# A fourth pair of heads turned through DRAM, other pairs in the output projection's parts, other weight forms: a two-layer decoder trunk on one core

## The chip, the core and the metric

The kernel runs on one core of one Trainium2 chip. The metric is device time in microseconds, the median over several executions. Engines are named as in the profile: PE is TensorE (matrix multiplication), PEld its loading of weights, DVE is VectorE, ACT is ScalarE, POOL is GpSimd, SP is SyncE, which here only issues DMAs.

## What is computed

Two decoder layers on 256 tokens of width 1024 (16 heads of 64), then one RMSNorm. Cut to what matters here:

```python
def reference(x, p, ...):
    h = x
    for i in range(DEPTH):                       # DEPTH = 2
        u = _rmsnorm(h, attn_norm_g[i])
        if i % 2 == 0:                           # layer 0: forgetting attention
            proj = u @ fox_w_in[0]               # q, k, v and the forget gates
            log_f = jax.nn.log_sigmoid(f_logit)
            o = _fox_attention(q, k, v, log_f)   # causal softmax(q.k/8 + c[t] - c[s]) v, c = cumsum(log_f)
            h = h + _merge_heads(o) @ fox_w_o[0]
        else:                                    # layer 1: MoBA; 256 tokens are one block, so it is causal
            proj = u @ moba_w_in[0]              # softmax(q.k/8 + T5 bias) v
            o = _moba_attention(q, k, v, rel_bias_table)
            h = h + _merge_heads(o) @ moba_w_o[0]
        u = _rmsnorm(h, ffn_norm_g[i])
        gu = u @ ffn_w_in[i]                     # 1024 -> 2 x 2816
        h = h + (jax.nn.silu(gu[..., :D_FF]) * gu[..., D_FF:]) @ ffn_w_out[i]
        gate = jax.nn.sigmoid(_rmsnorm(h, ple_norm_g[i]) @ ple_w_gate[i])
        h = h + gate * (p[i] @ ple_w_up[i])
    return _rmsnorm(h, final_norm_g)
```

All is in float32.

## The kernel before

**Products.** Activations lie with features on partitions: `[128, feature block, 256 tokens]`. A float32 product is made of three matmuls of a faster float32 type (`mm3`, L92 to L94): each operand is split into a rounded part `hi` and a remainder `lo`, and hi·hi, hi·lo and lo·hi are added up in a PSUM bank. A chunk of weights (512 KB) is 8 blocks of 128x128, and makes 24 matmuls.

**Weights** stream from DRAM in the order in which the host has laid them out, one chunk at a time, by SP's queue. ACT makes `whi` of a chunk (L164 or L182, one instruction), DVE makes the remainder `wlo` (L166 or L183). There are six buffers of each. A chunk lies in its buffers in one of three forms. Plain, `blocks()`: eight blocks one after the other, from column 16. Gapped, `gapped()`: the first block shifted by 8 columns and the seven others by 64, with 56 columns of zeros between, which come from DRAM with the chunk; `KICK` names the projection's parts that have it. Entry, `blocks(ENTRY)`: `whi` plain, and in `wlo` the first two blocks shifted by 8 and the others by 64, for which DVE makes two instructions of the remainder.

**Attention** (`attention`, the same code for both layers) goes by pairs of heads, 0 to 7. `project(j, 0)` and `project(j, 1)` make q and k of pair j into the bank `pq` (24 matmuls each). DVE scales them by the norm (`qkt`, L514); ACT and DVE split them (`qkh` L523, `qkl` L525). `scores` makes the logits `sp` of one or two pairs: in layer 0 a matmul with `sel` adds the decay (L372), then come q·k in three steps (L540, L543); DVE adds mask or bias and finds the minimum (L554), ACT takes the exponential (L558) into `e`. The probabilities must then be divided by their sum and transposed. There are two roads. For the pairs in `TURNED` = 0, 1, 3, ACT divides (`scaled`, L588, four instructions), DVE transposes 32x32 squares (`turn`, L595, two), POOL's queue writes the tile to DRAM (`dt`, L598) and reads it back in another order by four gathers (`pt`, L601). For the other pairs DVE divides (`normal`, L579, two), PE makes six transposes (`transposes`, L616), and ACT copies them out of PSUM (L623). Tiles `pt` of the DRAM road have two buffers, which a transposed pair without the tag "fp" uses too; the pairs with "fp" use four others. `values(...)` multiplies by v into a bank `po` per pair (L633, L635); ACT and DVE split the result into `o` (L285, L286).

**Order.** Pairs are projected two at a time, scores follow one pair behind, and the transposes and values of earlier pairs stand between a projection and the scores. Then comes the output projection `wo(hf, c)` in eight parts: half `hf` of the outputs, part `c` of the pairs of heads, part c taking the pairs 2c and 2c+1. Between parts stand what remains of the attention:

```
(0,0) | scores 7 | (1,0) | values 3, transposes 5 | (0,1) | transposes 6, 7 | (1,1) |
values 4 5, values 6 7 | (0,2) (1,2) (0,3) (1,3)
```

The program gives a priority by order of writing; `issue_after` and `held` put an instruction behind a named other one. Each engine runs its instructions in order. PSUM has eight banks, which all tiles of `bank(...)` take in turn, so a matmul into a new bank waits for whatever read that bank eight tiles earlier.

Of the kernel before, what the change touches and what calls it, by code (L numbers as in the profile page):

```python
# [32 lines left out]
P = 128  # L33
S = 256
D = 1024
KT = D // P
H = 16
DH = 64
NP = H // 2
DFF = 2816  # L40
FT = DFF // P
# [5 lines left out]
HW = 1024  # L47
HC = 512
# [1 line left out]
WARM = 8  # L50
RAW = 6
RVW = 384
TURNED = (0, 1, 3)


LINE = 64
# [2 lines left out]

FURTHER = 8  # L60
ENTRY = (0, 1)
KICK = ((0, 0), (0, 1), (1, 1), (0, 2))

GAP = LINE - FURTHER
WW = HW + GAP
# [8 lines left out]
def trunk(ctx: ExitStack, tc: tile.TileContext, xg, wx, xr, pt, w, cst, gf, rel, hot, rvm, out):  # L74
# [94 lines left out]
    def blocks(entry=()):  # L169

        hi, lo = half(APART, len(entry) * P)
        return [[t[k] if isinstance(t, list) else t[:, k * P:(k + 1) * P] for k in range(KT)] for t in (hi, lo)]
# [150 lines left out]
    moba = []  # L323
# [103 lines left out]
    def attention(layer, nm, mid, early, nf):  # L427
        vb = [bank(f"v{layer}_{b}") for b in range(4)]
        rest, ahead = None, []
        for c in range(4):  # L430
            wt = [early.pop(0) if early else half() for _ in range(2)]
# [59 lines left out]
        def project(j, a):  # L491
            with held(j - 2):
                if ahead:
                    hi, lo = ahead.pop(0)
                elif j > 2 and (j % 2 == 0 or layer and j == 5) and a == 0 or layer and j == 4:
                    hi, lo = gapped()
                else:
                    hi, lo = blocks(ENTRY if layer and j in (0, 2) and a == 0 else ())
            if a == 0:
                pq[j] = bank(f"pq{layer}_{j}")  # L500
            bk = pq[j]
            for k in range(KT):
                mm3(bk[:, a * S:(a + 1) * S], (hi[k], lo[k]), nm.k(k),
                    start=(k == 0), stop=(k == KT - 1))
            if a == 0:
                return
            del pq[j]
            far = [x for x in fresh if x[0] in TURNED]
            near = [x for x in fresh if x[0] not in TURNED]
            fresh.clear()  # L510
            for x in far:
                scaled(*x)
            t = work.tile([P, 2, S], F32, tag="qkt", bufs=3, name=f"qkt{layer}_{j}")
            got = nc.vector.tensor_tensor(t.rearrange("p a s -> p (a s)"), bk,  # L514
                                          nm.row.rearrange("p a s -> p (a s)"), op=ALU.mult)
            for x in near:
                with tc.issue_after(got.ins):
                    got = normal(*x)

            th = work.tile([P, 3 * P], F32R, tag="qkh", bufs=3, name=f"qkh{layer}_{j}")  # L520
            tl = work.tile([P, 3 * P], F32R, tag="qkl", bufs=3, name=f"qkl{layer}_{j}")
            src = t.rearrange("p a s -> p (a s)")[:, P:]
            first = nc.scalar.activation(th, src, AF.Copy)  # L523
            with tc.issue_after(got.ins):
                got = nc.vector.tensor_tensor(tl, src, f32(th), op=ALU.subtract)  # L525
            marks[j] = first, got
            qk[j] = t, th, tl
            for x in far:
                with tc.issue_after(got.ins):
                    turn(*x[:2])  # L530

        def scores(*js):

            rows = [slice(s * DH, (s + 1) * DH) for s in range(2)]
            heads = [(2 * j + s, d, qk[j], bank(f"sp{layer}_{2 * j + s}")) for j in js for s, d in enumerate(rows)]
            if add:
                for i, _, _, sp in heads:
                    add(i, sp)
            for _, d, (t, _, _), sp in heads:
                mm(sp[:, 0:P], t[d, 0, 0:P], t[d, 1, 0:P], start=add is None, stop=True, skip_group_check=True)  # L540
            for n, (q, k) in enumerate(((1, 1), (1, 2), (2, 1))):
                for _, d, t, sp in heads:
                    got = mm(sp[:, P:3 * P], t[q][d, 0:P], t[k][d, P:], start=False, stop=n == 2,  # L543
                             skip_group_check=True)
            sl = (slice(0, P), slice(P, 3 * P))
            for n, j in enumerate(js):
                del qk[j]
                e = work.tile([P, 2, 3 * P], F32, tag="e", bufs=4, name=f"e{layer}_{j}")

                mn = tiny.tile([P, 2, 2, 2], F32, tag="mn", bufs=4, name=f"mn{layer}_{j}")  # L550
                for s in range(2):
                    i, _, _, sp = heads[2 * n + s]
                    for q, b in enumerate(bias(i)):
                        nc.vector.tensor_tensor_reduce(e[:, s, sl[q]], sp[:, sl[q]], b, 1.0, 3.0e38,  # L554
                                                       ALU.add, ALU.min, mn[:, 0, s, q:q + 1])
                for s in range(2):
                    for q in range(2):
                        last = nc.scalar.activation(e[:, s, sl[q]], e[:, s, sl[q]], AF.Exp, scale=-1.0,  # L558
                                                    bias=mn[:, 0, s, q:q + 1], accum_out=mn[:, 1, s, q:q + 1])
                if j < NP - 3:  # L560
                    fresh.append((j, e, mn))
                else:
                    marks[-j] = last, normal(j, e, mn)
            return got
# [44 lines left out]
        def transposes(j, tag="pt"):  # L609

            e = sm.pop(j)
            for s in range(2):
                i = 2 * j + s
                pp = bank(f"pp{layer}_{i}")
                for q in range(3):
                    got = nc.tensor.transpose(pp[:, q * P:(q + 1) * P], e[:, s, q * P:(q + 1) * P], ident)  # L616
                if tag == "pt":
                    if s == 0:
                        both = work.tile([P, 2, 3 * P], F32, tag="pt", bufs=2, name=f"pt{layer}_{j}")
                    t = both[:, s]  # L620
                else:
                    t = work.tile([P, 2 * S], F32, tag="fp", bufs=4, name=f"pt{layer}_{i}")[:, 0:3 * P]
                nc.scalar.activation(t, pp[:, 0:3 * P], AF.Copy)  # L623
                pts[i] = t.rearrange("p (b c x) -> p b c x", b=3, x=32)
            return got

        def values(*js):

            pos = [bank(f"po{layer}_{j}") for j in js]
            heads = [(slice(s * DH, (s + 1) * DH), slice((2 * j + s) * DH, (2 * j + s + 1) * DH), pts.pop(2 * j + s), po)  # L630
                     for j, po in zip(js, pos) for s in range(2)]
            for d, c, t, po in heads:
                mm(po[d, :S], v[:, 0, c], t[:, 0:2], start=True, stop=False, skip_group_check=True)  # L633
            for d, c, t, po in heads:
                got = mm(po[d, P:S], v[:, 1, c], t[:, 2], start=False, stop=True, skip_group_check=True)  # L635
            for j, po in zip(js, pos):
                marks["o"] = split(oh[:, j], ol[:, j], po[:, :S])
            return got


        for j in range(0, NP, 2):
            for i in (j, j + 1):
                project(i, 0)
                project(i, 1)
            if j >= 4:
                transposes(j - 2, "fp")
                values(*range(max(j - 5, 0), j - 3))
            got = scores(*range(max(j - 1, 0), min(j + 1, NP - 1)))
            if layer == 0 and j == 0:
                with tc.issue_after(got.ins):  # L650
                    moba.extend(moba_bias())

        wb = [[bank(f"wo{layer}_{hf}_{b}") for b in range(2)] for hf in range(2)]

        def wo(hf, c, after):
            with held(after):
                wt = gapped() if (hf, c) in KICK else blocks()
            return cross(wb[hf], wt, (2 * c, 2 * c + 1), lambda k: (oh[:, k], ol[:, k]), 0, KT - 1, c == 3)

        def behind(ins, after, *parts):  # L660
            with tc.issue_after(ins.ins):
# [6 lines left out]
            end = scores(NP - 1)  # L668
        got = behind(end, 6, (1, 0))
        with tc.issue_after(got.ins):  # L670
            values(3)
            got = transposes(5, "fp")
        got = behind(got, 7, (0, 1))
        with tc.issue_after(got.ins):
            transposes(NP - 2)
            got = transposes(NP - 1)
        got = behind(got, -6, (1, 1))
        with tc.issue_after(got.ins):
            values(4, 5)
            got = values(6, 7)  # L680
        got = behind(got, -7, (0, 2), (1, 2))
        behind(got, "o", (0, 3))
# [268 lines left out]
def _gapped(a, first=0):  # L951

    t = a.reshape(P, KT, P)[:, _entered(first)].reshape(P, HW)
    return np.concatenate([t[:, :P], np.zeros((P, GAP), t.dtype), t[:, P:]], axis=1)


def _turned(a):

    t = a.reshape(a.shape[:-1] + (2, 4, 4, 32))
    return np.swapaxes(t, -3, -2).reshape(a.shape)  # L960
# [13 lines left out]

def _wide(a, c, hf):

    t = a[c * P:(c + 2) * P, hf * HC:(hf + 1) * HC]
    return t.reshape(2, P, HC).transpose(1, 0, 2).reshape(P, HW)


def _buckets():
# [84 lines left out]
```

## Time and profile before

| what | value |
|---|---|
| median of 3 executions | 647.32 us (647.26 to 648.54) |
| the profiled execution, its time | 647.72 us |
| its span in the trace | 645.9 us |
| its granted TensorE clock, mean | 0.996 |
| layer 0, from the projection of pair 2 to the end of the output projection | 41.9 to 115.1 us in the span |
| the same of layer 1 | 358.2 to 428.9 us |

Times of the trace are counted from the start of the span; the executions' times contain the span and 1.8 us around it. PE's busy time counts a matmul until its modelled end, and the next one starts before that: the durations of 0.28 us overlap, and what a matmul costs is the step from its start to the next start, some 0.12 us for 128x256. Where a row gives an instruction with "xN", its start is the first one's and its duration covers all N. In brackets stands how long the engine was idle before, and what it waited for.

### The profile page before, as it was taken

To read this page: it belongs to the slowest core of one execution; us is meant where nothing else is said; L and a number is where in the kernel's file an instruction comes from. 1 tells how busy PE (TensorE), PEld (TensorE's weight loads), DVE (VectorE), ACT (ScalarE), POOL (GpSimd) and SP (SyncE) were. 2 spreads that over 40 slices of the span, in tenths; PEclk is the share of its full clock that TensorE was granted. 3 is DMA by queue.
4 is the path that set the end of the run, shared out by engine and by line. 5 is a ranking of instruction groups with operands and counts; after the bars stand their busy time and mean duration, and the time that the engine had idled before them with its cause. 6 is when DMAs were issued, how large, how long until landed. Compare 5 with 4: busy or idle time off the path is not lost.

```text
span 645.9 us, 13154 instructions
## 1 busy us (share of the span) xinstructions
PE 636.6 (99%) x5321; PEld 614.3 (95%) x5321; DVE 454.7 (70%) x734; ACT 375.6 (58%) x645; POOL 26.6 (4%) x53
## 2 busy tenths in 40 slices
PE   9999999999999999999999999999999999999995
PEld 7899989999999999999989999999999999999984
DVE  6778885786666666668893798697666666666685
ACT  6677675764444444448664687676444444454653
POOL 0101110000000000000000031000000000000001
PEclk9999999999999999999999999999999999999998
DMA  8847665497765666665574587366766666666523
GB/s 333 315 137 212 201 181 155 166 332 270 247 202 198 197 195 214 196 206 180 189 247 176 176 251 217 106 232 205 222 198 199 198 196 191 195 207 189 189 97 100
DMA packets 39166, 131.06 MB, mean 203 GB/s; under 512 B 4576, under 2 KB 8640, under 8 KB 39104
## 3 DMA queue, kind: packets, MB, share of 16 engines
q1 hardware_dynamic: 37040, 124.87, 59.7%
q0 software_dynamic: 1632, 4.72, 2.5%
q8 instruction: 42, 0.69, 0.4%
q10 hardware_dynamic: 432, 0.62, 0.3%
q14 instruction: 20, 0.16, 0.1%
HBM read 125.71 MB, written 7.63 MB: 206 GB/s over the span
## 4 chain that ended last, share of the span: by engine, by line
PE 94%; issue 3%; DVE 1%; ACT 1%; POOL 0%; POOLq 0%; DVEq 0%; DMA 0%
PE gu L92 12%; PE gu L93 12%; PE gu L94 12%; PE fo L94 6%; PE fo L93 6%; PE fo L92 6%; PE pq L92 5%; PE pq L94 5%; PE pq L93 5%; PE v L423 4%; PE wo L92 2%; PE wo L93 2%; PE wo L94 2%; PE pg L92 2%; PE pg L93 1%
## 5 line engine op out<-in xcount | busy, mean ns | idle before, releaser
L166 DVE TENSOR_TENSOR wlo<-raw,whi 128x1024 fp32r<-128x1024 f32 (+1 forms) x166 | 200.5, 1216 | 71.3 <-ACT whi L164 65.8
L164 ACT ACTIVATE whi<-raw 128x1024 fp32r<-128x1024 f32 x164 | 172.0, 1057 | 103.4 <-issue 49.8
L92 PE MATMUL gu<-g,whi 128*128 128x256 f32 x704 | 195.2, 277 | 0.0
L93 PE MATMUL gu<-g,whi 128*128 128x256 f32 x704 | 194.9, 277 | 0.0
L94 PE MATMUL gu<-g,wlo 128*128 128x256 f32 x704 | 194.8, 277 | 0.0
L94 PEld LDWEIGHTS gu<-g,wlo 128*128 128x128 f32 x704 | 132.3, 188 | 0.0
L92 PEld LDWEIGHTS gu<-g,whi 128*128 128x128 f32 x704 | 132.3, 188 | 0.0
L93 PEld LDWEIGHTS gu<-g,whi 128*128 128x128 f32 x704 | 132.2, 188 | 0.0
L94 PE MATMUL fo<-fp,wlo 128*128 128x256 f32 x352 | 97.5, 277 | 0.0
L92 PE MATMUL fo<-fp,whi 128*128 128x256 f32 x352 | 97.4, 277 | 0.0
L93 PE MATMUL fo<-fp,whi 128*128 128x256 f32 x352 | 97.4, 277 | 0.0
L183 DVE TENSOR_TENSOR wlo<-raw,whi 128x1080 fp32r<-128x1080 f32 x44 | 55.9, 1275 | 29.7 <-ACT whi L182 29.1
L92 PE MATMUL pq<-g,whi 128*128 128x256 f32 x256 | 71.7, 280 | 0.0
L94 PE MATMUL pq<-g,wlo 128*128 128x256 f32 x256 | 71.0, 277 | 0.0
L93 PE MATMUL pq<-g,whi 128*128 128x256 f32 x256 | 71.0, 277 | 0.0
L93 PEld LDWEIGHTS fo<-fp,whi 128*128 128x128 f32 x352 | 66.2, 188 | 0.0
L92 PEld LDWEIGHTS fo<-fp,whi 128*128 128x128 f32 x352 | 66.1, 188 | 0.0
L94 PEld LDWEIGHTS fo<-fp,wlo 128*128 128x128 f32 x352 | 66.1, 188 | 0.0
L182 ACT ACTIVATE whi<-raw 128x1080 fp32r<-128x1080 f32 x44 | 48.1, 1100 | 27.5 <-PE gu L93 25.4
L92 PEld LDWEIGHTS pq<-g,whi 128*128 128x128 f32 x256 | 48.2, 188 | 1.0 <-issue 0.2
L93 PEld LDWEIGHTS pq<-g,whi 128*128 128x128 f32 x256 | 48.1, 188 | 0.1
L94 PEld LDWEIGHTS pq<-g,wlo 128*128 128x128 f32 x256 | 48.1, 188 | 0.0
(188 smaller groups left out, 999.9 us busy)
## 6 DMA issues: line engine op xcount, KB each, us to landing
raw<-w SPq DMA_DIRECT2D x169, 512.0 KB, 4.2
raw<-w SPq DMA_DIRECT2D x44, 540.0 KB, 4.5
d<-d SPq DMA_DIRECT2D x4, 768.0 KB, 7.0
dt<-turn POOLq DMA_DIRECT2D x6, 384.0 KB, 3.1
pt<-dt POOLq DMA_DIRECT2D x24, 96.0 KB, 5.3
bias<-d SPq DMA_DIRECT2D x4, 512.0 KB, 6.6
dh<-end SPq DMA_DIRECT2D x2, 512.0 KB, 2.6
ut<-dh SPq DMA_DIRECT2D x8, 128.0 KB, 3.2
```

Of the source, the lines that this page charges most:

```text
L92: mm(o, ah, bh, start=start, stop=False, skip_group_check=True)
L93: mm(o, ah, bl, start=False, stop=False, skip_group_check=True)
L94: return mm(o, al, bh, start=False, stop=stop, skip_group_check=True)
L164: state["hi"] = state[f"hi{i}"] = nc.scalar.activation(hi[:, c], raw[:, c], AF.Copy)
L166: nc.vector.tensor_tensor(lo[:, c], raw[:, c], f32(hi[:, c]), op=ALU.subtract)
L182: nc.scalar.activation(ht, raw[:, 0:WW], AF.Copy)
L183: nc.vector.tensor_tensor(lt, raw[:, 0:WW], f32(ht), op=ALU.subtract)
L423: got = mm(bks[2 * t + hf], x[a][:, t * P:(t + 1) * P], w[b][:, hf * HC:(hf + 1) * HC], start=k + a + b == 0, stop=k + b == KT, skip_group ...
```

## The change

Pair 2 joins the pairs that go through DRAM, in both layers. The projection's parts take the pairs 0 1, 2 4, 3 5 and 6 7; the host lays the weights out accordingly. The values of pair 4 move ahead of the last scores in the loop, behind those of pairs 1 and 2; the values of pair 3 move from between two parts to the place that pair 4 had, beside pair 5. The bias of layer 1 (one matmul `pb`, one DVE instruction, one DMA) moves from behind the first scores to ahead of them. Five chunks get other forms: `project(2, 0)` of layer 0 plain to entry; part (0,2) of layer 0 gapped to plain; parts (0,0) and (1,1) of layer 1 gapped to plain; part (0,2) of layer 1 gapped to entry. The transposes of pair 7 use the buffers "fp". Lines below L62 move down by one.

```diff
-TURNED = (0, 1, 3)
+TURNED = (0, 1, 2, 3)
...
-KICK = ((0, 0), (0, 1), (1, 1), (0, 2))
+KICK = (((0, 0), (0, 1), (1, 1)), ((0, 1),))
+PARTS = ((0, 1), (2, 4), (3, 5), (6, 7))
...
-                    hi, lo = blocks(ENTRY if layer and j in (0, 2) and a == 0 else ())
+                    hi, lo = blocks(ENTRY if (layer or j) and j in (0, 2) and a == 0 else ())
...
+            if layer + j == 0:
+                moba.extend(moba_bias())
             if j >= 4:
-                transposes(j - 2, "fp")
+                if j - 2 not in TURNED:
+                    transposes(j - 2, "fp")
                 values(*range(max(j - 5, 0), j - 3))
+            if j == NP - 2:
+                values(4)
             got = scores(*range(max(j - 1, 0), min(j + 1, NP - 1)))
-            if layer == 0 and j == 0:
-                with tc.issue_after(got.ins):
-                    moba.extend(moba_bias())
...
-                wt = gapped() if (hf, c) in KICK else blocks()
-            return cross(wb[hf], wt, (2 * c, 2 * c + 1), lambda k: (oh[:, k], ol[:, k]), 0, KT - 1, c == 3)
+                wt = gapped() if (hf, c) in KICK[layer] else blocks(ENTRY if layer and (hf, c) == (0, 2) else ())
+            return cross(wb[hf], wt, PARTS[c], lambda k: (oh[:, k], ol[:, k]), 0, KT - 1, c == 3)
...
         with tc.issue_after(got.ins):
-            values(3)
             got = transposes(5, "fp")
         got = behind(got, 7, (0, 1))
         with tc.issue_after(got.ins):
             transposes(NP - 2)
-            got = transposes(NP - 1)
+            got = transposes(NP - 1, "fp")
         got = behind(got, -6, (1, 1))
         with tc.issue_after(got.ins):
-            values(4, 5)
+            values(3, 5)
             got = values(6, 7)
...
 def _wide(a, c, hf):
 
-    t = a[c * P:(c + 2) * P, hf * HC:(hf + 1) * HC]
-    return t.reshape(2, P, HC).transpose(1, 0, 2).reshape(P, HW)
+    t = a.reshape(-1, P, D)[list(c), :, hf * HC:(hf + 1) * HC]
+    return t.transpose(1, 0, 2).reshape(P, HW)
```

**DVE at pair 4, layer 0.** In the rows, a name's last number only tells one tile from another; the number before it is the pair (`e_2` is pair 2), and for weights there is none. This is DVE before, from pair 4's `qkt` to pair 5's; `rc_2` is the reciprocal that pair 2 is divided by:

```order
L514 TENSOR_TENSOR qkt_4_773<-pq_4_712,row_326 128x512
L571 RECIPROCAL rc_2_775<-mn_2_697 128x4
L579 TENSOR_TENSOR e_2_696<-e_2_696,rc_2_775 128x2x128
L579 TENSOR_TENSOR e_2_696<-e_2_696,rc_2_775 128x2x256
L525 TENSOR_TENSOR qkl_4_780<-qkt_4_773,qkh_4_779 128x384
L595 STREAM_TRANSPOSE turn_1_783<-e_1_686 128x3x4x32 x2
L183 TENSOR_TENSOR wlo_925<-raw_923,whi_924 128x1080
L166 TENSOR_TENSOR wlo_956<-raw_954,whi_955 128x1024
L514 TENSOR_TENSOR qkt_5_854<-pq_5_799,row_326 128x512
L525 TENSOR_TENSOR qkl_5_857<-qkt_5_854,qkh_5_856 128x384
```

And now:

```order
L572 RECIPROCAL rc_2_774<-mn_2_698 128x4
L515 TENSOR_TENSOR qkt_4_780<-pq_4_713,row_326 128x512
L526 TENSOR_TENSOR qkl_4_783<-qkt_4_780,qkh_4_782 128x384
L596 STREAM_TRANSPOSE turn_1_786<-e_1_687 128x3x4x32 x2
L596 STREAM_TRANSPOSE turn_2_796<-e_2_697 128x3x4x32 x2
L184 TENSOR_TENSOR wlo_926<-raw_924,whi_925 128x1080
L167 TENSOR_TENSOR wlo_957<-raw_955,whi_956 128x1024
L515 TENSOR_TENSOR qkt_5_867<-pq_5_812,row_326 128x512
L287 TENSOR_TENSOR o_369<-po_0_873,o_369 128x256
L526 TENSOR_TENSOR qkl_5_870<-qkt_5_867,qkh_5_869 128x384
```

The two dividing instructions of pair 2 are gone from ahead of `qkl_4`, and its two turns stand ahead of the next weights' remainder; on ACT four divisions of pair 2 now stand ahead of `qkh_4`.

**POOL, layer 0.** This is the queue of the DRAM road before, for pairs 1 and 3:

```order
L598 DMA dt_1_786<-turn_1_783 128x768
L601 DMA pt_1_788<-dt_1_786 32x4x192 x4
L598 DMA dt_3_1003<-turn_3_1000 128x768
L601 DMA pt_3_1005<-dt_3_1003 32x4x192 x4
L243 TENSOR_TENSOR col_1632<-ms_1630,nhalf 128x2
```

And now:

```order
L599 DMA dt_1_789<-turn_1_786 128x768
L599 DMA dt_2_799<-turn_2_796 128x768
L602 DMA pt_1_791<-dt_1_789 32x4x192 x4
L602 DMA pt_2_801<-dt_2_799 32x4x192 x4
L599 DMA dt_3_1004<-turn_3_1001 128x768
L602 DMA pt_3_1006<-dt_3_1004 32x4x192 x4
```

Pair 2's copy out stands between pair 1's copy and its gathers, and pair 2's gathers behind those.

**PE at the projection's first part, layer 0.** This is the change of bank within part (0,0) before, with the semaphores that an instruction waits for ("Activation" is ACT; `wo0_0_0` is layer 0, half 0, bank 0):

```order
L94 MATMUL wo0_0_0_1155<-o0_369,wlo24_1161 128x256
L92 MATMUL wo0_0_1_1156<-o0_369,whi24_1160 128x256 [waits Activation_49]
L93 MATMUL wo0_0_1_1156<-o0_369,whi24_1160 128x256
L94 MATMUL wo0_0_1_1156<-o0_369,wlo24_1161 128x256
L92 MATMUL wo0_0_1_1156<-o0_369,whi24_1160 128x256
```

And now:

```order
L95 MATMUL wo0_0_0_1163<-o0_369,wlo24_1169 128x256
L93 MATMUL wo0_0_1_1164<-o0_369,whi24_1168 128x256 [waits DVE_49]
L94 MATMUL wo0_0_1_1164<-o0_369,whi24_1168 128x256
L95 MATMUL wo0_0_1_1164<-o0_369,wlo24_1169 128x256
L93 MATMUL wo0_0_1_1164<-o0_369,whi24_1168 128x256
```

The second bank is six matmuls behind the first, and is now freed by DVE where an ACT eviction freed it.

More of the change, by code (lines that the diff above doesn't have):

```diff
@@ L1012 @@
                 for n, a in enumerate(_cols(wi[:, :D], wi[:, D:2 * D]))]
-        seq += [_gapped(_wide(wo, 2 * c, hf)) if (hf, c) in KICK else _wide(wo, 2 * c, hf)
+        seq += [_gapped(_wide(wo, PARTS[c], hf)) if (hf, c) in KICK[i] else _wide(wo, PARTS[c], hf)
                 for hf, c in ((0, 0), (1, 0), (0, 1), (1, 1), (0, 2), (1, 2), (0, 3), (1, 3))]
@@ L1024 @@
                 seq += o[f - 2:f]
-        seq.append(_wide(fout[i], FT - 4, 0))
+        seq.append(_wide(fout[i], (FT - 4, FT - 3), 0))
         seq += _rows(_turned(ar(ple_w_up)[i]) if i else ar(ple_w_up)[i])
-        seq += [_wide(fout[i], f, hf) for f, hf in ((FT - 2, 0), (FT - 4, 1), (FT - 2, 1))]
-        a = [_wide(_turned(ar(ple_w_gate)[i]) if i else ar(ple_w_gate)[i], 2 * c, hf) for hf in range(2) for c in range(4)]
+        seq += [_wide(fout[i], (f, f + 1), hf) for f, hf in ((FT - 2, 0), (FT - 4, 1), (FT - 2, 1))]
+        a = [_wide(_turned(ar(ple_w_gate)[i]) if i else ar(ple_w_gate)[i], (2 * c, 2 * c + 1), hf) for hf in range(2) for c in range(4)]
         seq += a if i else [_gapped(t) for t in a]
```

## The prediction

> **What bounds the kernel now.** I read the page's busy times and its chain first, then who waited for whom on TensorE, then windows by stage of the attention, and last the timelines of TensorE (PE), VectorE (DVE), ScalarE (ACT) and GpSimd (POOL) around the places that the diff touches.
>
> ```profile
> PE 636.6 (99%) x5321; PEld 614.3 (95%) x5321; DVE 454.7 (70%) x734; ACT 375.6 (58%) x645; POOL 26.6 (4%) x53
> PE 94%; issue 3%; DVE 1%; ACT 1%; POOL 0%; POOLq 0%; DVEq 0%; DMA 0%
> PE wo L92 <- ACT o L285: 0.5, 1, 0.5
> PE wo L93 <- DVE o L286: 0.3, 1, 0.3
> ```
>
> PE is busy for 99% of the span and carries 94% of the chain that ends last, so the time is the sum of PE's rows plus the few places where PE waits. Only one place of any size is listed: the output projection, once for ACT's half and once for DVE's half of an attention output `o`. A change pays here if it takes rows off PE or takes a wait away, and costs if it gives PE a new wait. Whether it can do the latter is told by how full the helpers are where the change adds work:
>
> ```profile
> 69.38:84.31 14.93, 14.93 (x145) 14.16 (x143) 12.33 (x31) 10.93 (x30) 1.34 (x3) 1.00 0.69 200
> 103.72:115.14 11.42, 11.42 (x99) 11.42 (x97) 10.63 (x15) 9.20 (x14) 0.00 (x0) 1.00 0.64 208
> ```
>
> These are layer 0's stage of pairs 6 and 7, and the projection's last four parts (columns: length, PE, weight loads, DVE, ACT, POOL, clock, DMA share, GB/s). DVE has 12.33 of 14.93 us filled in the first and 10.63 of 11.42 in the second: it runs close behind PE, and late work on it is caught up slowly.
>
> **The weight form of pair 2, layer 0.** Layer 1 already has there, behind the same kind of score matmuls, the "entry" form that layer 0 now gets.
>
> ```profile
> 41.91 0.39 PE L92 MATMUL pq<-g,whi 128*128 128x256 f32 x1
> 53.20 0.28 PE L94 MATMUL pq<-g,wlo 128*128 128x256 f32 x1
> 53.41 0.62 PE L372 MATMUL sp<-c,sel 64*128 64x384 f32 x4
> 358.22 0.39 PE L92 MATMUL pq<-g,whi 128*128 128x256 f32 x1
> 369.33 0.72 PE L540 MATMUL sp<-qkt 64*128 64x128 f32 x8
> ```
>
> The 96 matmuls of pairs 2 and 3 take 41.91 to 53.41 = 11.50 us in layer 0, and 358.22 to 369.33 = 11.11 us in layer 1. I take the whole difference, -0.39 (ends 0 and -0.5). The bias matmul `pb`, which now stands ahead of the first scores and no longer between them and pair 2, takes there what it took here and costs nothing anew; its one DVE instruction moves with it, in a stage where DVE is not yet behind. The second DVE instruction that an entry remainder takes falls there too, and in layer 1 into part (0,2), ahead of which DVE has stood idle while PE makes the values.
>
> **Pair 2 leaves TensorE, in both layers.**
>
> ```profile
> 66.01 0.28 PE L94 MATMUL pq<-g,wlo 128*128 128x256 f32 x1
> 66.13 0.82 PE L616 MATMUL pp<-con,e 128*128 128x128 f32 x6
> 66.88 0.65 PE L633 MATMUL po<-pt,v 128*64 128x256 f32 x4
> 67.68 0.62 PE L372 MATMUL sp<-c,sel 64*128 64x384 f32 x4
> ```
>
> Six transposes fill 66.13 to 66.88 = 0.75. A projection that ends before a 64-row matmul needs 0.21 for its last step (53.20 to 53.41) where it needs 0.12 before a transpose (66.01 to 66.13), so 0.09 comes back: -0.66 a layer, -1.32 in all (ends -1.2 and -1.5). The Trainium skill, in "VectorE: DVE Perf Modes", section "The three transpose paths", gives 390 ns for a 128x128 transpose on TensorE and advises TensorE for this size; by that figure twelve of them would be 4.7 us and the sum below nearer -5.9. The trace has 0.125 us each here, and the trace decides.
>
> **Values regrouped.** Pair 3 no longer stands alone between two parts of the projection; pair 4 joins pairs 1 and 2, and pair 3 takes pair 4's old place.
>
> ```profile
> 81.15 1.08 PE L633 MATMUL po<-pt,v 128*64 128x256 f32 x8
> 82.60 0.62 PE L372 MATMUL sp<-c,sel 64*128 64x384 f32 x4
> 91.13 0.65 PE L633 MATMUL po<-pt,v 128*64 128x256 f32 x4
> 91.93 0.88 PE L616 MATMUL pp<-con,e 128*128 128x128 f32 x6
> ```
>
> Alone, a pair takes 0.80 (91.13 to 91.93; 0.80 too at 66.88 to 67.68) and another 0.09 at the edge. Two together take 1.45, so a further one 0.65. Net -0.25 a layer, -0.50 in all (ends -0.3 and -0.7). Pair 4's evictions must be done by then; the six transposes lie 1.45 us of value matmuls ahead, more than ACT's two evictions take.
>
> **The wait in projection part (0,1).** Its second half needs `o` of pair 3, whose value matmuls ran just before.
>
> ```profile
> 93.95 0.28 PE L94 MATMUL wo<-o,wlo 128*128 128x256 f32 x1
> 94.70 0.39 PE L92 MATMUL wo<-o,whi 128*128 128x256 f32 x1 [0.46 <-ACT o L285]
> 95.37 0.39 PE L93 MATMUL wo<-o,whi 128*128 128x256 f32 x1 [0.28 <-DVE o L286]
> 408.91 0.28 PE L92 MATMUL wo<-o,whi 128*128 128x256 f32 x1
> 409.09 0.39 PE L93 MATMUL wo<-o,whi 128*128 128x256 f32 x1
> 409.31 0.28 PE L94 MATMUL wo<-o,wlo 128*128 128x256 f32 x1
> ```
>
> Steps are 0.12 elsewhere in this part; here they are 0.75 and 0.67 in layer 0 (1.18 too long) and 0.18 and 0.22 in layer 1 (0.16 too long). With pairs 2 and 4 the part needs only outputs that are some 7 us old. I take -1.34 (ends -1.1 and -1.5). Next in line are pairs 3 and 5 for part (0,2), behind two value groups as pairs 4 and 5 were, so nothing is late there that was not before.
>
> **What the helpers pay.** Pair 2's scaling goes from DVE to ACT: four more instructions ahead of `qkh` of pair 4, and DVE turns two pairs before it splits the next weights.
>
> ```profile
> 60.75 1.48 ACT L588 ACTIVATE e<-e,rc 128x128 f32<-128x128 f32 x4
> 62.13 0.51 ACT L523 ACTIVATE qkh<-qkt 128x384 fp32r<-128x384 f32 x1
> 63.15 1.03 DVE L595 STREAM_TRANSPOSE turn<-e 128x384 f32<-128x384 f32 x2
> 64.11 1.24 DVE L183 TENSOR_TENSOR wlo<-raw,whi 128x1080 fp32r<-128x1080 f32 x1
> 67.97 0.56 DVE L525 TENSOR_TENSOR qkl<-qkt,qkh 128x384 fp32r<-128x384 f32 x1 [0.89 <-ACT qkh L523]
> 75.16 0.69 DVE L514 TENSOR_TENSOR qkt<-pq,row 128x512 f32<-128x512 f32 x1 [1.28 <-PE pq L94]
> 84.31 0.39 PE L92 MATMUL wo<-o,whi 128*128 128x256 f32 x1
> 84.45 0.75 DVE L286 TENSOR_TENSOR o<-po,o 128x256 fp32r<-128x256 f32 x2
> ```
>
> Four scalings take 62.13 - 60.75 = 1.38, so `qkh`, `qkl` and the first turn come 1.38 later; the second turn adds 64.11 - 63.15 = 0.96. The two normalizing instructions that DVE loses stood ahead of `qkl`, in time that DVE now spends waiting for ACT, so they give nothing back. The weight remainder at 64.11 is thus 2.34 later, 1.95 with the 0.39 that pair 2's form gains. DVE makes up for it out of its idle 0.89 at 67.97 (two evictions of pair 2 no longer stand ahead of that `qkh`) and by one weight remainder that the new order puts behind the score operations, into the 1.28 idle at 75.16; I count some 0.34 left, and from there on DVE has almost no idle time until the projection. What it hits is a PSUM bank. The banks go round by eight, and with three value banks for two, and two transposes' banks gone, the projection's second bank now is the one that DVE's split of pair 1 frees (before, an ACT eviction freed it). That split, the first of the two at 84.45, ended some 0.41 later at 84.86 and now ends at 85.20. PE reaches the first part at 84.31 - 0.39 - 0.66 + 0.65 = 83.91 and the bank six matmuls on, 0.22 and five times 0.12 later, at 84.73: a new wait of 0.47, say 0.5.
>
> ```profile
> 399.25 0.38 PE L92 MATMUL wo<-o,whi 128*128 128x256 f32 x1
> 399.73 0.75 DVE L286 TENSOR_TENSOR o<-po,o 128x256 fp32r<-128x256 f32 x2
> ```
>
> In layer 1 the bank is wanted at 399.25 - 0.66 + 0.65 + 0.82 = 400.06 and was free at 400.14 before. PE has no `sel` matmuls there (the row at 67.68 is one of these groups), so the helpers have less time to catch up: I put the split 0.5 late, which is a wait of 0.6, and 0.1 for pair 7's weights. Together +1.2; the ends are 0 (all caught up) and 2.7 (1.95 late in layer 0 leaves more standing).
>
> **Other weight forms.** Layer 1's parts (0,0) and (1,1) and both tails from (0,2) lose or change the gap. Both tails run at 11.42/96 = 0.119 us a matmul where others have 0.116 or less. Back at that pace a tail would save 0.3 to 0.5, but DVE fills 10.63 of the 11.42, so the feed-forward part would start no more than some 0.1 or 0.2 sooner. I take -0.15 for all four (ends +0.2 and -0.9).
>
> **The road through DRAM.** Per layer five more DMAs on POOL's queue: pair 2's copy out goes between pair 1's copy and its four gathers, and pair 2's gathers stand behind those.
>
> ```profile
> 64.47 0.56 POOL L598 DMA_DIRECT2D dt<-turn  x1 [7.96 <-DVE turn L595]
> 67.64 2.18 POOL L601 DMA_DIRECT2D pt<-dt  x4 [2.60 <-DMA dt<-turn]
> 384.23 2.18 POOL L601 DMA_DIRECT2D pt<-dt  x4 [3.20 <-DMA dt<-turn]
> 396.44 1.08 PE L633 MATMUL po<-pt,v 128*64 128x256 f32 x8
> DMA to landing us min/median/max: 4.0/5.3/6.9
> ```
>
> Layer 0: the copy of pair 1 issues at 64.47 + 1.38 - 0.39 = 65.46, pair 1's gathers at 68.63 to 70.81, pair 2's at 70.81 to 72.99, landed by 79.9 at the slowest; PE wants them at 81.15 - 1.05 = 80.10. Layer 1: issued 384.23 + 1.38 + 2.18 = 387.79 to 389.97, landed at 395.3 in the median and 396.9 at worst, wanted at 396.44 - 0.66 + 0.1 = 395.9. I cost it at nothing; its cover is 0.2 at worst in layer 0 and 0.6 in the median in layer 1, and up to 1.0 if that is gone. Pair 3's gathers now wait for pair 1's buffer too, but are wanted some 10 us later than before.
>
> **Sum.** -0.39 - 1.32 - 0.50 - 1.34 + 1.2 - 0.15 = -2.5 us on the profiled execution of 647.72 (span 645.9 and 1.8 around it). That execution lies 0.40 above the median of 647.32; the change is in the span, so I carry -2.5 to the median: **644.8**.
>
> **Rivals.** (a) The helpers' lateness is not caught up, and the bank waits eat the gain: DVE's fullness speaks for it, its idle 0.89 and 1.28 against. With the upper end of 2.7 for 1.2 the time is 646.3, no measurable change. (b) The paces and the lateness both fall well: helper waits at 0.3 and the tails at full gain give 647.32 - 0.39 - 1.32 - 0.50 - 1.34 + 0.3 - 0.9 = 643.2. (c) The new form at pair 2 does not do in layer 0 what it does in layer 1: without its 0.39 and with nothing from the other forms, 645.3. (d) Slower: pair 2's probabilities come too late for the value matmuls of pairs 1 and 2, and PE stands there in both layers. It costs as much as the landing overshoots 80.1 and 395.9, and decides when the two overshoot by 2.5 together. If each of the eight gathers of pairs 1 and 2 were held up by one DVE instruction of 1.2, pair 2 would be 9.6 later, some 9 us would stand out per layer, and the time were about 662. Against it: the four gathers at 67.64 issued in 2.18, 0.55 each, while DVE worked without a break beside them but for 0.89. The Trainium skill, "SBUF — State Buffer", section "SBUF: two separate sides", warns of exactly this (descriptors of POOL's DMAs blocked by VectorE on a shared port); the 0.55 here shows no such blocking.
>
> **Chances.** Forecast 0.62, (a) 0.11, (b) 0.11, (c) 0.12, (d) 0.04. 0.2% is 1.3 us, about what a measurement of this kernel can tell from no change. Faster by more: forecast, (b), (c) and a little of (a), 0.86; within: the rest of (a), 0.10; slower 0.04. The range leaves out (d), half of (a) and the edge of (b): 643.6 to 646.1.
>
> **What would show it.** Pairs 2 and 3 of layer 0 in 11.1; no transposes behind pair 5; part (0,1) of layer 0 in some 3.0 for 4.19 without a wait on `o`; in the first part of each projection a wait of about half a microsecond, six matmuls in, ended by DVE's `o`. If that wait is over 1 us, or the first value matmul of pair 2 is released by a DMA, or DVE's `qkl` of pair 4 is late by much more than 1.4, the forecast is too low.

## The result

The changed kernel takes 644.25 us (median of 5, 644.07 to 645.16) beside 648.36 of the kernel before in the same group of runs: ratio 0.9947, interval 0.9932 to 0.9961. In a later group it took 644.45 beside 647.53: 0.9951 (0.9937 to 0.9964). Against the 647.32 on which the prediction stood that is -3.1; forecast were -2.5, 644.8, and 643.6 to 646.1. The kernel before took 647.52 to 647.55 in three later groups, so its 648.36 is high, and the gain is some 3.1 to 3.3 us, 0.5%. One execution of the later group took 3646 us and one of share_dve below took 1646; the ratios leave both out.

The profiled execution's span went from 645.9 to 642.5. Of these -3.4, -0.59 lie ahead of pair 2's first matmul in layer 0, which starts at 41.91 before and at 41.32 after. They are there already at the layer's first projection (29.77 and 29.19), ahead of anything that was changed. Over all profiles of this study the start of pair 2 lies between 41.29 and 42.19 and follows no edit; both profiles of the changed kernel have 41.32, and what sets it was not found. So every profile is compared below from that matmul to the end of the span: **603.99 before, 601.18 after, -2.81**. The spans are read to 0.1, so such a difference is good to about 0.1.

### The profile page after: what moved, and what is told of

The parts are those of the page before. It is cut to its first block, busy times and chain, and to the rows that moved or that the text cites. A ratio compares the mean times of both kernels' runs of the same rounds, so it can differ in the third digit from the quotient of the medians.

```text
span 642.5 us, 13152 instructions
## 1 busy us (share of the span) xinstructions
PE 632.9 (99%) x5309; PEld 611.4 (95%) x5309; DVE 454.2 (71%) x736; ACT 376.9 (59%) x649; POOL 32.3 (5%) x63
## 4 chain that ended last, share of the span: by engine, by line
PE 82%; DVE 4%; issue 4%; ACT 4%; DMA 3%; POOL 1%; POOLq 0%; DVEq 0%; ACTq 0%
PE gu L94 13%; PE gu L93 12%; PE gu L95 12%; PE fo L95 6%; PE fo L94 6%; PE fo L93 6%; PE v L424 4%; PE wo L93 2%; PE pq L93 2%; PE wo L94 2%; PE wo L95 2%; PE pq L95 2%; PE pq L94 2%; DMA pt<-dt 2%; PE pg L93 2%
## 5 line engine op out<-in xcount | busy, mean ns | idle before, releaser
L167 DVE TENSOR_TENSOR wlo<-raw,whi 128x1024 fp32r<-128x1024 f32 (+1 forms) x168 | 202.9, 1215 | 71.7 <-ACT whi L165 65.9
L165 ACT ACTIVATE whi<-raw 128x1024 fp32r<-128x1024 f32 x166 | 174.1, 1056 | 103.3 <-issue 49.6
L184 DVE TENSOR_TENSOR wlo<-raw,whi 128x1080 fp32r<-128x1080 f32 x40 | 50.8, 1275 | 28.6 <-ACT whi L183 28.6
L183 ACT ACTIVATE whi<-raw 128x1080 fp32r<-128x1080 f32 x40 | 43.7, 1101 | 26.4 <-PE gu L94 25.4
```

Of the source, the lines that this page charges most:

```text
L165: state["hi"] = state[f"hi{i}"] = nc.scalar.activation(hi[:, c], raw[:, c], AF.Copy)
L167: nc.vector.tensor_tensor(lo[:, c], raw[:, c], f32(hi[:, c]), op=ALU.subtract)
L183: nc.scalar.activation(ht, raw[:, 0:WW], AF.Copy)
L184: nc.vector.tensor_tensor(lt, raw[:, 0:WW], f32(ht), op=ALU.subtract)
```

## The profile after

The page: the span, two of the engines, and the chain that ended last.

```profile
span 642.5 us, 13152 instructions
PE 632.9 (99%) x5309; PEld 611.4 (95%) x5309; DVE 454.2 (71%) x736; ACT 376.9 (59%) x649; POOL 32.3 (5%) x63
PE 82%; DVE 4%; issue 4%; ACT 4%; DMA 3%; POOL 1%; POOLq 0%; DVEq 0%; ACTq 0%
```

PE has lost 3.7 us of busy time and twelve matmuls. The chain, 94% PE before, now leaves PE: where PE waits for a bank, the page follows it back through DVE, ACT and the DMAs (DVE itself shows no wait for a DMA there). PE's waits name the place (us in total, times, longest):

```profile
PE wo L93 <- DVE o L287: 0.7, 2, 0.4
```

That is the wait that was forecast, once in each layer; the waits of 0.5 and 0.3 for `o` in part (0,1) are gone. PE's timeline in layer 0 (start, duration, operation, tiles), the first row of each stage:

```profile
41.32 0.38 PE L93 MATMUL pq<-g,whi 128*128 128x256 f32 x1
52.45 0.44 PE L373 MATMUL sp<-c,sel 64*128 64x384 f32 x2
54.15 0.39 PE L93 MATMUL pq<-g,whi 128*128 128x256 f32 x1
65.25 0.65 PE L634 MATMUL po<-pt,v 128*64 128x256 f32 x4
66.05 0.61 PE L373 MATMUL sp<-c,sel 64*128 64x384 f32 x4
79.52 1.08 PE L634 MATMUL po<-pt,v 128*64 128x256 f32 x8
80.87 0.60 PE L634 MATMUL po<-pt,v 128*64 128x256 f32 x4
81.62 0.61 PE L373 MATMUL sp<-c,sel 64*128 64x384 f32 x4
83.32 0.38 PE L93 MATMUL wo<-o,whi 128*128 128x256 f32 x1
84.03 0.28 PE L95 MATMUL wo<-o,wlo 128*128 128x256 f32 x1
84.62 0.39 PE L93 MATMUL wo<-o,whi 128*128 128x256 f32 x1 [0.32 <-DVE o L287]
91.24 0.36 PE L93 MATMUL wo<-o,whi 128*128 128x256 f32 x1
94.06 0.49 PE L617 MATMUL pp<-con,e 128*128 128x128 f32 x3
```

Pairs 2 and 3 take 52.45 - 41.32 = 11.13 for 11.50 (11.12 by unrounded starts, as in the table below). At 65.25 values follow where six transposes stood. The three value pairs take 81.62 - 79.52 = 2.10. In part (0,0) the seventh matmul starts 0.59 behind the sixth, where 0.12 is the step. Part (0,1) takes 94.06 - 91.24 = 2.82 for 4.19. Layer 1:

```profile
386.89 0.28 PE L94 MATMUL pq<-g,whi 128*128 128x256 f32 x1
387.14 0.38 PE L95 MATMUL pq<-g,wlo 128*128 128x256 f32 x1
397.36 0.28 PE L95 MATMUL wo<-o,wlo 128*128 128x256 f32 x1
397.99 0.38 PE L93 MATMUL wo<-o,whi 128*128 128x256 f32 x1 [0.35 <-DVE o L287]
414.26 0.39 PE L93 MATMUL wo<-o,whi 128*128 128x256 f32 x1
425.27 0.28 PE L93 MATMUL gu<-g,whi 128*128 128x256 f32 x1
425.60 0.39 PE L94 MATMUL gu<-g,whi 128*128 128x256 f32 x1
```

The first two rows are a wait for pair 7's `wlo` (0.25 for a step of 0.11), the next two the bank. The tail takes 425.27 - 414.26 = 11.01 for 11.41, and then the feed-forward part's first step is 0.33, waiting for `g`. What the helpers do behind pair 4 in layer 0:

```profile
59.79 2.87 ACT L589 ACTIVATE e<-e,rc 128x128 f32<-128x128 f32 x8
62.56 0.51 ACT L524 ACTIVATE qkh<-qkt 128x384 fp32r<-128x384 f32 x1
63.10 0.56 DVE L526 TENSOR_TENSOR qkl<-qkt,qkh 128x384 fp32r<-128x384 f32 x1 [2.43 <-ACT qkh L524]
63.58 1.95 DVE L596 STREAM_TRANSPOSE turn<-e 128x384 f32<-128x384 f32 x4
84.16 1.08 DVE L287 TENSOR_TENSOR o<-po,o 128x256 fp32r<-128x256 f32 x3
68.84 4.37 POOL L602 DMA_DIRECT2D pt<-dt  x8 [2.46 <-DMA dt<-turn]
```

ACT makes eight divisions ahead of `qkh`, DVE waits 2.43 for it, and only then turns both pairs. POOL issues the eight gathers in 4.37, 0.55 each, while DVE is busy for 3.79 of the 4.37.

The stages in which before and after differ, from a stage's first matmul to the next one's (us):

| stage | layer 0 before, after | layer 1 before, after |
|---|---|---|
| pairs 2 and 3 | 11.50, 11.12 | 11.11, 11.11 |
| pairs 4 and 5, and the transposes behind them | 11.77, 11.11 | 11.83, 11.17 |
| pairs 6 and 7 | 11.02, 11.02 | 11.02, 11.26 |
| values ahead of the loop's last scores | 1.45, 2.10 | 1.45, 2.10 |
| part (0,0) | 2.95, 3.56 | 3.03, 3.56 |
| part (1,0), then values of 3 and transposes of 5 | 4.35, 3.41 | 4.35, 3.51 |
| part (0,1) | 4.19, 2.82 | 3.06, 2.84 |
| part (1,1) | 2.99, 2.90 | 3.00, 2.91 |
| the last four parts, then the first 72 of the feed-forward | 19.64, 19.63 | 19.62, 19.51 |

The rows add up to -2.7. What follows the 72 matmuls of layer 1, which no edit touches, took 208.7 to 209.1 over all profiles, so differences of less than 0.5 to the end of the span say little by themselves; the stages say more.

## The experiments

Each row's last column is the time from pair 2's first matmul to the end of the span in the profile, 603.99 before and 601.18 after (after_again is the changed kernel once more, in the group of dve_scale, share_dve and double_turn). The ratio is to the kernel before in the same group. The profiled execution of old_parts, 651.23, was the slowest of its six.

| kernel | median | ratio to before | to the end |
|---|---|---|---|
| no_entry | 644.94 | 0.9956 (0.9944 to 0.9969) | 601.14 |
| pb_only | 647.11 | 0.9994 (0.9986 to 1.0003) | 603.83 |
| pb_back | 644.89 | 0.9962 (0.9949 to 0.9974) | 601.51 |
| turned_only | 649.38 | 1.0027 (1.0018 to 1.0036) | 605.41 |
| parts_only | 645.28 | 0.9965 (0.9951 to 0.9978) | 602.11 |
| old_parts | 649.40 | 1.0031 (1.0020 to 1.0043) | 607.96 |
| old_forms | 644.92 | 0.9962 (0.9950 to 0.9975) | 601.73 |
| after_again | 644.45 | 0.9951 (0.9937 to 0.9964) | 601.28 |
| share | 643.77 | 0.9940 (0.9926 to 0.9953) | 600.18 |
| dve_scale | 643.12 | 0.9931 (0.9918 to 0.9943) | 599.95 |
| share_dve | 643.25 | 0.9930 (0.9917 to 0.9944) | 600.02 |
| double_turn | 645.49 | 0.9966 (0.9954 to 0.9978) | 601.98 |

**What made pairs 2 and 3 of layer 0 faster: the form, or the place of `pb`?** Three kernels fill the table of the two edits.

```diff
no_entry, against the changed kernel:
-  blocks(ENTRY if (layer or j) and j in (0, 2) and a == 0 else ())
+  blocks(ENTRY if layer and j in (0, 2) and a == 0 else ())
pb_only, against the kernel before (pb_back is the reverse, against the changed one):
+            if layer + j == 0:
+                moba.extend(moba_bias())
             ...
             got = scores(*range(max(j - 1, 0), min(j + 1, NP - 1)))
-            if layer == 0 and j == 0:
-                with tc.issue_after(got.ins):
-                    moba.extend(moba_bias())
```

> The changed kernel, but project(2, 0) of layer 0 has plain weights again; nothing else differs. Theory A (the form sets PE's pace): the 96 matmuls of pairs 2 and 3 of layer 0 go from 11.12 us back to 11.50, and the span from 642.5 to 642.9. Theory B (the pace came from moving the bias matmul pb from directly ahead of pair 2 to ahead of the scores): they stay at 11.1 and the span at 642.5.

> The kernel before with one edit alone: the bias matmul pb, its DVE instruction and its DMA stand ahead of the first scores of layer 0. Plain weights at pair 2, as before. Theory A (moving pb gave pairs 2 and 3 of layer 0 their faster pace): their 96 matmuls go from 11.50 to 11.1 us, span 645.9 - 0.4 = 645.5. Theory B (the pace there needs the other edits as well, such as another state of PE on entry): 11.5, span 645.9.

> The changed kernel with pb, its DVE instruction and its DMA back behind the first scores, directly ahead of pair 2; the entry form of pair 2 stays. Theory A (the pace comes from where pb stands, and the form does nothing): 11.12 goes to 11.5, span 642.9. Theory B (either of the two edits is enough; with pb ahead of pair 2 the entry form's gap brings the fast pace after eight matmuls, as in layer 1's other entry chunks): 11.1 to 11.15, span 642.5.

Pair 2's first matmul and the first score matmul behind pair 3, PE's timeline. Without the entry form, `pb` moved:

```profile
41.66 0.38 PE L93 MATMUL pq<-g,whi 128*128 128x256 f32 x1
52.76 0.44 PE L373 MATMUL sp<-c,sel 64*128 64x384 f32 x2
```

The kernel before with `pb` moved alone:

```profile
41.77 0.38 PE L92 MATMUL pq<-g,whi 128*128 128x256 f32 x1
52.87 0.44 PE L372 MATMUL sp<-c,sel 64*128 64x384 f32 x2
```

The changed kernel with `pb` back ahead of pair 2, the entry form kept:

```profile
41.92 0.34 PE L393 MATMUL pb<-hot,rr 64*128 64x384 f32 x1
42.19 0.38 PE L93 MATMUL pq<-g,whi 128*128 128x256 f32 x1
53.69 0.44 PE L373 MATMUL sp<-c,sel 64*128 64x384 f32 x2
```

11.10, 11.10 and 11.50. With the changed kernel's 11.12 and the 11.50 of before, the pace follows `pb` in all four cells, and the form does nothing there. In the time, 0.4 us is too little for the intervals; it is the rows that decide.

**What pair 2's road is worth alone, and the new parts alone.** turned_only is the kernel before with `TURNED = (0, 1, 2, 3)` and the transposes of pair 2 left out; parts_only is the kernel before with `PARTS`, `values(4)` and `values(3, 5)` and the buffers of pair 7 as in the change; old_parts is the changed kernel with the parts and values of before.

> The kernel before with one edit alone: pair 2 through DRAM in both layers. Theory A (terms as predicted and seen): twelve transposes with their edges are -1.32; no bank wait arises, since the banks stand as before; helpers run up to 2 us later, which costs about 0.2 at pair 7's weights in layer 1; the wait in part (0,1) stays: span 645.9 - 1.1 = 644.8. Theory B (the helpers' lateness costs more than a bank): the gain is under 0.5, span above 645.4, and PE waits for qkl, weights or o at places where it didn't before.

> The kernel before with the parts and values of the changed one, alone: parts of pairs 0 1, 2 4, 3 5, 6 7, values(4) ahead of the last scores of the loop, values(3, 5) later, pair 7's transposes in the other buffers. Pair 2 stays on TensorE, the weight forms and pb stay. Theory A: values -0.5; the wait for o in part (0,1) goes, -1.3 to -1.5; the new bank wait in part (0,0) comes without any lateness of the helpers from pair 2, so under 0.5 a layer (PE comes 0.65 later, the bank's reader as before): 0.1 to 0.3 each; span 645.9 - 1.5 = 644.4. Theory B (the bank wait is as large as in the changed kernel, because it is the third value pair that makes it): 0.6 and 0.5, span 645.0.

> The changed kernel with the parts and values of before: parts take pairs 0 1, 2 3, 4 5, 6 7; values(3) alone ahead of part (0,1), values(4, 5) later. Pair 2 stays on the DRAM road, the forms stay. Theory A (the new wait in part (0,0) is for the PSUM bank that the third value pair put there): the waits in (0,0) vanish in both layers (3.56 to about 3.0), the wait for o in part (0,1) of layer 0 comes back (2.82 to about 4.2), values cost 0.5 more: span 642.5 + 0.5 + 1.5 - 1.1 = 643.4. Theory B (the wait in (0,0) is the helpers' lateness from pair 2's divisions and turns, whatever the bank): it stays, and the span is about 644.5.

turned_only is slower than before: theory B, and beyond it, since no gain is left at all. The transposes go as forecast (11.11 and 11.17 where 11.77 and 11.83 stood), but part (0,1) grows from 4.19 to 5.03 in layer 0 and from 3.06 to 3.60 in layer 1, (0,0) by 0.23 and 0.42, and some 0.6 more is lost at scores, weights and (1,0). ACT and PE in layer 0 there:

```profile
93.76 0.28 PE L94 MATMUL wo<-o,wlo 128*128 128x256 f32 x1
95.35 0.38 PE L92 MATMUL wo<-o,whi 128*128 128x256 f32 x1 [1.31 <-ACT o L285]
93.99 1.04 ACT L164 ACTIVATE whi<-raw 128x1024 fp32r<-128x1024 f32 x1
94.94 0.36 ACT L285 ACTIVATE o<-po 128x256 fp32r<-128x256 f32 x1
```

PE reaches the need for pair 3's `o` as early as before or earlier, ACT reaches its eviction 0.65 later (94.94 for 94.29); the two weight copies ahead of it stand there before, too, and start 0.64 later themselves (93.99 for 93.35 in the second), so ACT has carried its lateness this far. parts_only makes -1.88 of the -2.81 by itself. Its part (0,0) takes 2.95 and 2.93: no bank wait without pair 2's lateness. So turned_only +1.42, parts_only -1.88 and pb_only's stage -0.40 add up to -0.9; together they make -2.8. Of the missing 1.9, some 1.4 lie in the two attentions and the 72 matmuls behind each. The waits on a fresh `o` in part (0,1), 0.84 and 0.54, which lateness adds in the old parts and cannot add in the new ones, are as much by themselves. The other losses that the changed kernel does not have (0.4 in turned_only at scores and part (1,0), 0.3 in parts_only at layer 0's feed-forward) are for the most part made up by its larger loss in part (0,0), 0.61 and 0.53 where turned_only has 0.23 and 0.42. The last 0.5 lie behind layer 1's attention, within the scatter given above. old_parts was meant as the same test from the other side and is no clean one: it kept pair 7's transposes in the buffers "fp", which pair 4 still holds until its later values, and PE waits 0.8 for ACT's `pt` there; part (0,1) of layer 0 took 5.25.

**Bank or lateness?** share puts the values of pairs 1 and 2 into one bank; dve_scale lets DVE divide pair 2; share_dve does both.

```diff
share:
+            if js == (1, 2):
+                both = bank(f"po{layer}_1")
+                pos = [both[:, n * S:n * S + S] for n in range(2)]
...
-                mm(po[d, :S], v[:, 0, c], t[:, 0:2], start=True, ...)
+                mm(po[d, :S], v[:, 0, c], t[:, 0:2], start=n < 2 or js != (1, 2), ...)
dve_scale:
-            near = [x for x in fresh if x[0] not in TURNED]
+            near = [x for x in fresh if x[0] not in TURNED or x[0] == 2]
...
             for x in far:
-                scaled(*x)
+                if x[0] != 2:
+                    scaled(*x)
```

> The changed kernel, but the values of pairs 1 and 2 share one PSUM bank (256 columns each), so that two banks hold the three pairs and the projection's second bank is one that PE and ACT left long before. Theory A (bank): no wait six matmuls into (0,0); the next need of pair 1's o is six matmuls further on, 0.7 us later, when it is ready; (0,0) takes about 3.0 for 3.56 in both layers, span 642.5 - 1.0 = 641.5, time about 643.2. Theory B (lateness, not the bank): the wait only moves six matmuls on, to the first use of pair 1's o, and the span stays within 0.2 of 642.5.

> The changed kernel, but pair 2 is divided by DVE (reciprocal and two multiplications, as before the change) and not by four ACT instructions, in both layers; it still goes through DRAM. Theory A (the helpers' lateness comes from ACT's four divisions ahead of qkh of pair 4, during which DVE stands idle 2.4 us, so that DVE can divide at no cost): qkl of pair 4, the turns and all gathers come 1.0 to 1.4 earlier, the bank waits in part (0,0) shrink from 0.61 and 0.53 to under 0.2 each, the wait for pair 7's weights in layer 1 goes; from pair 2's first matmul to the end 601.2 - 1.0 = 600.2. Theory B (the lateness is DVE's own, from the two turns): DVE gets 1.0 more work, the waits stay or grow, 601.2 or more.

> The changed kernel with both: pairs 1 and 2 share a value bank, and DVE divides pair 2. Theory A: no wait on banks as in the shared version, pair 7's weights in layer 1 in time (-0.2), the road of pair 2 with about 1 us to spare: from pair 2's first matmul to the end 600.0, some 1.2 less than the changed kernel, time about 643. Theory B (sharing had taken all there was): 600.2, as the shared version.

> The changed kernel once more, as the reference of this group. From pair 2's first matmul to the end 601.2 in the profile; the start before that may differ by up to 0.9, as it did between the runs so far (41.3 to 42.2).

share: part (0,0) takes 2.95 and 2.92 for 3.56, as theory A has it, and PE has no wait left in the projection. 0.2 of the gain is lost elsewhere: layer 1's last four parts ran at 11.41 again and not at 11.01, with the same weight forms. dve_scale has the same 2.95 and 2.92 with the changed kernel's banks, and pair 7's weights in time (11.00 for 11.26). ACT and DVE behind pair 4 of layer 0 in dve_scale:

```profile
60.01 1.48 ACT L590 ACTIVATE e<-e,rc 128x128 f32<-128x128 f32 x4
61.40 0.51 ACT L525 ACTIVATE qkh<-qkt 128x384 fp32r<-128x384 f32 x1
60.96 1.03 DVE L581 TENSOR_TENSOR e<-e,rc 128x256 f32<-128x256 f32 x2
61.94 0.56 DVE L527 TENSOR_TENSOR qkl<-qkt,qkh 128x384 fp32r<-128x384 f32 x1
62.41 1.95 DVE L597 STREAM_TRANSPOSE turn<-e 128x384 f32<-128x384 f32 x4
83.04 1.08 DVE L287 TENSOR_TENSOR o<-po,o 128x256 fp32r<-128x256 f32 x3
```

PE there, the sixth and the seventh matmul of part (0,0), with the step of 0.12 and no wait:

```profile
84.25 0.28 PE L95 MATMUL wo<-o,wlo 128*128 128x256 f32 x1
84.37 0.28 PE L93 MATMUL wo<-o,whi 128*128 128x256 f32 x1
```

DVE's two multiplications lie in time in which it waited for ACT; `qkl` has no wait there, and counted from pair 2's first matmul (41.55 and 41.32) it starts at 20.39 for 21.78. DVE's `o` ahead of part (0,0) is as much earlier, 41.49 for 42.84. So neither the third value bank (parts_only) nor the lateness (share) makes the wait for the bank alone, and it is ACT's four divisions that make the lateness. Lateness alone costs something else: the 0.23 and 0.42 of turned_only in part (0,0) come where pair 1's new `o` is first used, behind the twelfth matmul, in layer 1 as a wait of 0.20 on DVE's `o`, with slower steps after it. dve_scale, 643.12, has the lowest median of all, 1.3 under the changed kernel in the same group (0.9931 and 0.9951, whose intervals just overlap; its slowest execution, 643.63, lies below the changed kernel's fastest, 644.19; 1.3 too from pair 2 to the end); with the shared bank on top (643.25) nothing more is to be had.

**The road through DRAM, and the lateness doubled.** double_turn lets DVE turn pair 1 twice.

```diff
-            for s in range(2):
+            for s in (0, 1, 0, 1) if j == 1 else (0, 1):
                 nc.vector.transpose(...)
```

> The changed kernel, but DVE turns pair 1 twice (two transposes more, same data, in both layers), which puts pair 1's copy out, all eight gathers of pairs 1 and 2 and the DVE work behind it 0.96 us later. Theory A (in layer 0 pair 2's road has no spare time left; in one run of this study PE waited 0.3 for it): the value matmuls of layer 0 wait about 0.9 for pair 2's gathers, and PE then finds the bank of part (0,0) as before; layer 1 has about 1 us to spare on the road and pays at the bank instead, up to 0.9. Together +1.2 to +1.8, span measured from pair 2's first matmul 601.2 to about 602.7. Theory B (the road has spare time and the helpers catch up): under +0.5.

Neither theory holds as written. It costs 0.8 in all, but layer 0 pays 0.1 at the bank and nothing at the gathers. That does not show spare time on the road: counted from pair 2's first matmul the copies went out 0.91 later (24.50 for 23.59), but pair 1's landed sooner, so that the gathers began only 0.13 later (27.65 for 27.52). Nor is DVE's `o` ahead of part (0,0) late by the added 0.96: it starts 0.08 later than in the changed kernel (84.94 - 42.02 for 84.16 - 41.32). So in layer 0 more work of DVE at this place is caught up, and more work of ACT, by dve_scale, is not. Layer 1 pays at pair 7's weights, in PE's timeline:

```profile
388.07 0.28 PE L94 MATMUL pq<-g,whi 128*128 128x256 f32 x1
388.76 0.39 PE L95 MATMUL pq<-g,wlo 128*128 128x256 f32 x1 [0.41 <-DVE wlo L167]
```

The 96 matmuls take 12.26 for 11.26, and with PE that much later the bank is free: (0,0) takes 2.94; the feed-forward part starts 0.3 slower. Here one lateness is paid once, at the first place that is tight. That the road in layer 0 has little to spare was seen elsewhere, in old_forms:

```profile
80.27 0.65 PE L634 MATMUL po<-pt,v 128*64 128x256 f32 x4
81.27 0.65 PE L634 MATMUL po<-pt,v 128*64 128x256 f32 x4 [0.35 <-DMA pt<-dt]
```

Pair 2's values stand 0.5 behind there; its gathers took up to 7.9 us to land, 7.0 in the changed kernel's profile, where PE did not wait. How often that happens was not tried.

**The projection's weight forms.** old_forms is the changed kernel with `KICK` of before in both layers.

> The changed kernel with the projection's weight forms of before in both layers: parts (0,0), (0,1), (1,1) and (0,2) gapped. Theory A (the forms of the projection were worth what the stages show): layer 1's last four parts go from 11.01 back to 11.4, the feed-forward part after it, which waited 0.3 for the norm's g, gets that back; together under 0.3 slower, span 642.5 to 642.8. Theory B (the forms mean nothing here, paces fall as PE happens to enter a stage): no stage changes by more than 0.1 except by chance, and one that was slow may be fast.

Layer 1's tail is slow again (11.41, then 8.21), as theory A has it. But parts_only, with the same forms, has 11.02 and then 8.50 there, the changed kernel's figures with the new forms; and layer 0's tail became fast in both, 11.02 for 11.41, and lost by it. So it is theory B: the pace does not follow the form. The first matmuls of the feed-forward part in parts_only:

```profile
112.37 0.28 PE L93 MATMUL gu<-g,whi 128*128 128x256 f32 x1
112.83 0.38 PE L94 MATMUL gu<-g,whi 128*128 128x256 f32 x1 [0.18 <-DVE g L205]
113.05 0.28 PE L95 MATMUL gu<-g,wlo 128*128 128x256 f32 x1
113.17 0.28 PE L93 MATMUL gu<-g,whi 128*128 128x256 f32 x1
```

PE waits for the norm's `g`, and the 72 matmuls then take 8.92 for 8.22: tail and feed-forward together 19.94, 0.3 more than with the slow tail.

## Why the prediction was right, and where it was not

- **Weight form of pair 2, -0.39: right size by luck, wrong cause.** The stage gave -0.38, because the change moves `pb` as well. The step that failed is the bias matmul that "takes there what it took here and costs nothing anew": moving it is the whole effect, and the form has none. I had compared layer 0 with layer 1 and seen one difference, the form; there was a second, that layer 0 alone had a matmul of another shape directly ahead of the stage. Rival (c) had the form right and the time wrong.
- **Transposes, -1.32: right.** -0.66 in each layer. The Trainium skill's 390 ns a transpose ("VectorE: DVE Perf Modes", "The three transpose paths") would have made -4.7 of it. The page gives it for bf16; the step in this trace's rows of float32 transposes is 0.125, and that is what held.
- **Values regrouped, -0.50: right.** +0.65 at the loop's end and, with the edges at part (1,0), -0.94 and -0.84 behind it: -0.29 and -0.19.
- **Wait in part (0,1), -1.34:** -1.37 and -0.22, in all -1.59; some 0.2 of it is that the part's 24 steps run at 0.113 for 0.118.
- **What the helpers pay, +1.2: right in place and size.** Part (0,0) grew by 0.61 and 0.53, of which the waits six matmuls in, ended by DVE's `o`, are 0.47 and 0.51 over the usual step; with +0.24 at pair 7's weights that is 1.38. But where I had the lateness from ACT's divisions and DVE's turn together, with the divisions taken off ACT nothing is left of the waits, and with DVE's turns doubled layer 0 paid 0.1. The prediction saw that DVE's lost multiplications would give nothing back, since DVE waits for ACT there; it did not conclude that they were better left on DVE.
- **Other forms, -0.15:** the tail of layer 1 -0.40, the feed-forward part behind it +0.29, as the sentence on DVE's 10.63 of 11.42 had it; with -0.09 at each (1,1), -0.3. The size is near by luck, for the term is not a property of the form. Part (1,1) of layer 0 kept its form and gained the same 0.09; parts_only, with all forms of before, has 2.90 and 2.91 at (1,1) and 11.02 for layer 1's tail; and share has 11.41 with the new forms.
- **The road, 0: right.** In layer 0 the last gather landed at 79.4 (issued at 72.7, 6.7 to landing), 0.1 ahead of the first value matmul at 79.52, where 0.2 was worked out; pair 2's own come 0.5 behind that one, which the prediction left out. The gathers issued in 0.55 each beside a working DVE, so nothing here speaks for (d). The Trainium skill ("SBUF — State Buffer", "SBUF: two separate sides") has the blocking for VectorE instructions in a two-port mode; no view here tells an instruction's mode, so the trace shows only that those beside the gathers did not block them, and not that the rule is wrong.
- **The sum** came to -2.81 for -2.5, and the start gave 0.59 more, for which the prediction had no term. The terms added up only because the edits came together: the sum took the wait in (0,1) as it was before, 1.18 and 0.16, and let the new parts remove it. Had I asked what pair 2's road does without them, that wait would have grown by 0.84 and 0.54, and the first half of the change would have been a loss, as turned_only is.

## What to carry to other kernels

Where helpers run close behind the main engine, price an edit that makes them later at every place that uses their newest output; moving those uses to older outputs can be worth more than the work that is taken off, and the two belong into one change. Move work to the engine that stands idle at that moment, not to the one that is idle on average: ACT is at 59% and DVE at 71%, and yet the divisions belonged on DVE. Where two places run at different paces, list all differences between them before one is named the cause, and undo each alone.

## What the runs showed of the hardware that was not expected

The same 128x256 matmuls run at one of two steps for a whole stage but its first few, 0.113 or 0.118 us, at a granted clock of 1.00. In the one stage where a single edit was tried, pairs 2 and 3 of layer 0, what ran just ahead set it (with `pb` there 11.50 for 96, without it 11.10); elsewhere it fell either way with the same forms and order (layer 1's tail 11.01 in the changed kernel, 11.41 in share). What decides it was not found.
